# Rotary embedding on one core: alignment instructions on two engines, and the first batch's stores cut 4, 12 and 16 KB

## The chip, the cores and the metric

The kernel runs on one core of a Trainium2 chip. A core has TensorE (PE), VectorE (DVE), ScalarE (ACT), GpSimd (POOL) and SyncE (SP), and 16 DMA engines that move data between HBM and the on-chip memory. The metric is the device time of one execution in microseconds (us); smaller is better. Before the change the median of three runs is 163.62 us (163.49 to 163.76).

## The reference

```python
def reference(x, cos, sin):
    x1 = x[..., : x.shape[-1] // 2]
    x2 = x[..., x.shape[-1] // 2 :]
    cos = cos[None, :, None, :]
    sin = sin[None, :, None, :]
    out1 = x1 * cos - x2 * sin
    out2 = x1 * sin + x2 * cos
    return np.concatenate([out1, out2], axis=-1)
```

`x` is 8 x 2048 x 8 x 64 (batch, position, head, width) in float32, 33.55 MB; `cos` and `sin` are 2048 x 32. Each head's two halves are rotated by the angle of its position. Every element is read once and written once.

## The kernel before

**Tiling.** Each of the 8 batches is one tile `xt`, 128 partitions by 8192 elements: a partition holds 16 consecutive positions, 32 KB in one contiguous row of HBM. There are five such buffers (`NBUF`); the result is written over the input in the same buffer, and stored from there. `HD` is 512 elements (2 KB, one position), `UNIT` is 2048 elements (8 KB, four positions).

**Loads.** All go to SyncE's queue (lines 66 to 69). Batch 0 comes in three parts, with rows of 8, 8 and 16 KB, and the cosine table after the first of them; every later batch is one transfer of 128 rows of 32 KB. The sine table is the first transfer of ScalarE's queue (line 76). The loads of batches 0 to 4 are issued at the start, and the load of batch b + 5 after batch b in the program, where it waits for the store of batch b, whose buffer it takes.

**Work.** `rotate` handles one piece, usually 2048 columns. GpSimd makes the sine products in two instructions (line 122), VectorE the cosine products in one (line 129), and for most pieces (kind A) VectorE adds the two (line 136). For five first pieces of a batch (kinds B and C) TensorE adds through an identity matrix `eye`, and ScalarE copies the sum back (lines 143 to 168); in kind C VectorE makes the sine products as well (line 148). `eye` is made by GpSimd at the start (lines 80 and 81), and ScalarE derives the negated tables from it and from the sine table (lines 90 to 92).

**Stores.** Batches 0 to 6 are stored through ScalarE's queue, batch 7 through SyncE's (line 73). Batch 0 is computed in pieces of 2, 2, 4, 4 and 4 positions (`pieces`), and stored in two transfers (`shares`), the first when 4096 columns are done, that is after its third piece. Batches 1 to 6 are one store each, with rows of 32 KB. Batch 7 is stored in three transfers, with rows of 16, 8 and 8 KB.

**Order.** Nearly every instruction is wrapped in `keep`, so each engine runs them in the order of the program text. The semaphores that tell of a transfer's landing are eight and are handed out in rotation, so that some transfers wait for an earlier one with the same semaphore.

Of the kernel before, what the change touches and what calls it, by code (L numbers as in the profile page):

```python
# [10 lines left out]
def kernel(  # L11
# [7 lines left out]
    nc = tc.nc  # L19
    keep = tc.keep_in_program_order  # L20
# [6 lines left out]
    HD = H * D  # L27
    R = S // P
    ROW = R * HD
    UNIT = 4 * HD  # L30
# [20 lines left out]
    eye = const_pool.tile([P, P], f32, tag="eye")  # L51
# [25 lines left out]
    for b in range(NBUF):  # L77
        load(b)

    nc.gpsimd.memset(eye, 0.0)  # L80
    nc.gpsimd.affine_select(
        out=eye,
        in_=eye,
# [92 lines left out]

    def shares(b):
        if b == 0:
            return [2 * UNIT, 2 * UNIT]
        if b == last:  # L180
            return [2 * UNIT, UNIT, UNIT]
        return [ROW]

    for b in range(B):
        done = 0
        outs = list(spans(shares(b)))
        for lo, n in spans(pieces(b)):
            rotate(b, lo, n)
            done = lo + n
            while outs and sum(outs[0]) <= done:  # L190
                store(b, *outs.pop(0))
        if b + NBUF <= last:
            load(b + NBUF)
# [30 lines left out]
```

## Time and profile before

| quantity | value |
|---|---|
| median of 3 runs | 163.62 us |
| span of the profiled execution, first to last instruction | 161.8 us |
| what the median has beyond the span | 1.8 us |
| read from HBM, written to HBM | 34.08 MB, 33.55 MB |
| mean rate over the span | 418 GB/s |
| VectorE's last addition ends | 156.02 us |

The time of the profiled execution itself is not given apart from its span, so the difference of 1.8 us stands for what lies before and after it. In the chain of work that ended last, the transfers have 48% of the span, VectorE 37%, GpSimd 9%:

```profile
DMA 48%; DVE 37%; POOL 9%; issue 2%; DVEq 0%; SPq 0%; POOLq 0%; ACTq 0%
```

The main groups of instructions are GpSimd's two products and VectorE's product and addition. The columns are line, engine, operation, output and inputs, count; then busy time and mean length in ns; then the engine's idle time before them and what ended it:

```profile
L122 POOL TENSOR_TENSOR t<-xt,sin_sb 128x1024 f32<-128x1024 f32 (+1 forms) x32 | 70.4, 2199 | 13.5 <-DMA xt<-in_x_dram 8.3
L129 DVE TENSOR_TENSOR t<-xt,cos_ps 128x2048 f32<-128x2048 f32 (+1 forms) x34 | 73.4, 2167 | 0.8
L136 DVE TENSOR_TENSOR xt<-t,t 128x2048 f32<-128x2048 f32 (+1 forms) x29 | 62.2, 2145 | 8.2 <-POOL t L122 5.5
```

The transfers by issuing queue, with the size of each and the median time from issue to landing:

```profile
xt<-in_x_dram SPq DMA_DIRECT2D x7, 4096.0 KB, 42.8
out_dram<-xt ACTq DMA_DIRECT2D x6, 4096.0 KB, 27.2
out_dram<-xt ACTq DMA_DIRECT2D x2, 2048.0 KB, 22.3
out_dram<-xt SPq DMA_DIRECT2D x1, 2048.0 KB, 9.9
out_dram<-xt SPq DMA_DIRECT2D x2, 1024.0 KB, 6.2
```

### The profile page before, as it was taken

The numbers are of one execution on the slowest core, as the hardware profiler recorded it, in microseconds if no ns is written. First come the engines' busy times: TensorE is split into PE (matmuls) and PEld (weight loads), VectorE is DVE, ScalarE is ACT, GpSimd is POOL, SyncE is SP. The second block draws the span as 40 slices with busy tenths as digits, with TensorE's granted clock in tenths as the row PEclk, the third lists the DMA queues.
The fourth block names the chain that finished last, engine by engine and source line by source line (L and its number), as shares of the span: only waits on it lengthen the run. The fifth ranks groups of instructions, "written<-read, shape, count | busy, mean of one in ns | idle before, by whom it ended". The sixth has DMA issues, their size and how long they took to land.

```text
span 161.8 us, 459 instructions
## 1 busy us (share of the span) xinstructions
PE 49.4 (31%) x80; PEld 18.5 (11%) x80; DVE 140.1 (87%) x66; ACT 12.8 (8%) x14; POOL 138.9 (86%) x70
## 2 busy tenths in 40 slices
PE   0000000597309760978049714972000000000000
PEld 0000000142004220322023301330000000000000
DVE  0297999999999999999999999199989999899950
ACT  3300000002200220021000220022000000000000
POOL 1399997998999999992999959999899997999800
PEclk9999999999975998589957995699655555555555
DMA  5999999999999999899899999999999999999995
GB/s 158 425 454 494 413 308 446 413 470 405 462 405 462 389 502 405 389 510 397 389 510 397 389 512 397 397 502 397 397 488 413 405 478 413 405 478 409 397 419 225
DMA packets 3314, 67.65 MB, mean 418 GB/s; under 512 B 368, under 2 KB 368, under 8 KB 624
## 3 DMA queue, kind: packets, MB, share of 16 engines
q1 hardware_dynamic: 2016, 38.01, 55.5%
q10 hardware_dynamic: 1296, 29.62, 42.6%
q14 instruction: 2, 0.02, 0.0%
HBM read 34.08 MB, written 33.55 MB: 418 GB/s over the span
## 4 chain that ended last, share of the span: by engine, by line
DMA 48%; DVE 37%; POOL 9%; issue 2%; DVEq 0%; SPq 0%; POOLq 0%; ACTq 0%
DMA xt<-in_x_dram 26%; DVE t L129 18%; DMA out_dram<-xt 18%; DVE xt L136 17%; POOL t L122 9%; DMA sin_sb<-in_sin_dram 4%; DVE t L148 1%; DVEq L136 0%; SPq L67 0%; POOLq L122 0%; ACTq L74 0%
## 5 line engine op out<-in xcount | busy, mean ns | idle before, releaser
L122 POOL TENSOR_TENSOR t<-xt,sin_sb 128x1024 f32<-128x1024 f32 (+1 forms) x32 | 70.4, 2199 | 13.5 <-DMA xt<-in_x_dram 8.3
L129 DVE TENSOR_TENSOR t<-xt,cos_ps 128x2048 f32<-128x2048 f32 (+1 forms) x34 | 73.4, 2167 | 0.8
L122 POOL TENSOR_TENSOR t<-xt,nsin 128x1024 f32<-128x1024 f32 (+1 forms) x32 | 70.3, 2196 | 0.0
L136 DVE TENSOR_TENSOR xt<-t,t 128x2048 f32<-128x2048 f32 (+1 forms) x29 | 62.2, 2145 | 8.2 <-POOL t L122 5.5
L143 PE MATMUL o<-t,eye 128*128 128x512 f32 x24 | 17.0, 799 | 23.1 <-DVE t L129 19.6
L160 PE MATMUL o<-t,eye 128*128 128x512 f32 x16 | 12.0, 844 | 37.8 <-DVE t L129 35.6
L144 PE MATMUL o<-t,eye 128*128 128x512 f32 x24 | 14.9, 709 | 0.0
L145 ACT COPY xt<-o 128x1024 f32<-128x1024 f32 x6 | 6.1, 1012 | 45.7 <-PE o L144 45.7
L143 PEld LDWEIGHTS o<-t,eye 128*128 128x128 f32 x24 | 5.5, 256 | 32.5 <-issue 26.5
L160 PEld LDWEIGHTS o<-t,eye 128*128 128x128 f32 x16 | 3.7, 256 | 43.2 <-issue 39.4
L165 ACT COPY xt<-o 128x1024 f32<-128x1024 f32 x4 | 4.0, 1012 | 47.8 <-PE o L161 47.8
L93 DVE COPY cos_ps<-cos_sb 128x512 f32<-128x512 f32 x1 | 0.7, 695 | 6.9 <-DMA cos_sb<-in_cos_dram 6.9
L144 PEld LDWEIGHTS o<-t,eye 128*128 128x128 f32 x24 | 5.6, 234 | 8.2 <-issue 7.6
L161 PE MATMUL o<-t,neye 128*128 128x512 f32 x8 | 6.3, 875 | 0.2
L148 DVE TENSOR_TENSOR t<-xt,sin_ps 128x2048 f32<-128x2048 f32 x2 | 4.6, 2281 | 0.0
L161 PE MATMUL o<-t,eye 128*128 128x512 f32 x8 | 4.1, 592 | 0.0
L161 PEld LDWEIGHTS o<-t,neye 128*128 128x128 f32 x8 | 2.2, 300 | 5.3 <-issue 3.6
L161 PEld LDWEIGHTS o<-t,eye 128*128 128x128 f32 x8 | 1.5, 190 | 1.9 <-issue 1.9
L90 ACT ACT_TABLE_LOAD x1 | 1.3, 1283 | 1.2 <-PEq L208 1.2
L90 ACT ACTIVATE nsin<-sin_sb 128x512 f32<-128x512 f32 x1 | 0.6, 629 | 4.0 <-DMA sin_sb<-in_sin_dram 4.0
L91 ACT COPY sin_ps<-sin_sb 128x512 f32<-128x512 f32 x1 | 0.6, 580 | 0.0
L80 POOL MEMSET eye<- 128x128 f32 x1 | 0.2, 204 | 0.3 <-POOLq L208 0.3
(6 smaller groups left out, 1.0 us busy)
## 6 DMA issues: line engine op xcount, KB each, us to landing
xt<-in_x_dram SPq DMA_DIRECT2D x7, 4096.0 KB, 42.8
out_dram<-xt ACTq DMA_DIRECT2D x6, 4096.0 KB, 27.2
out_dram<-xt ACTq DMA_DIRECT2D x2, 2048.0 KB, 22.3
xt<-in_x_dram SPq DMA_DIRECT2D x2, 1024.0 KB, 6.7
xt<-in_x_dram SPq DMA_DIRECT2D x1, 2048.0 KB, 12.2
out_dram<-xt SPq DMA_DIRECT2D x1, 2048.0 KB, 9.9
out_dram<-xt SPq DMA_DIRECT2D x2, 1024.0 KB, 6.2
sin_sb<-in_sin_dram ACTq DMA_DIRECT2D x1, 256.0 KB, 5.7
```

Of the source, the lines that this page charges most:

```text
L90: keep(nc.scalar.mul(nsin, sin_sb, -1.0))
L93: keep(nc.vector.tensor_copy(cos_ps, cos_sb))
L122: nc.gpsimd.tensor_mul(out=t2u[:, :, u, :].rearrange("p (r h) d -> p r h d", h=H), in0=xu[:, :, 1 - u, :].rearrange("p (r h) d -> p r h d" ...
L129: nc.vector.tensor_mul(out=t1.rearrange("p (r k d) -> p r k d", r=nr, d=Dh), in0=xk, in1=rep(cos_ps[:, r0 : r0 + nr, :], 2 * H),)
L136: keep(nc.vector.tensor_add(out=xt, in0=t1, in1=t2))
L143: nc.tensor.matmul(oc, eye, t1[:, cs], start=True, stop=False)
L144: nc.tensor.matmul(oc, eye, t2[:, cs], start=False, stop=True)
L145: keep(nc.scalar.copy(xt[:, 2 * j * C : 2 * (j + 1) * C], o))
L148: nc.vector.tensor_mul(out=t2.rearrange("p (r k d) -> p r k d", r=nr, d=Dh), in0=xk, in1=rep(sin_ps[:, r0 : r0 + nr, :], 2 * H),)
L160: nc.tensor.matmul(oc, eye, t1u[:, gs, u, :], start=True, stop=False)
L161: nc.tensor.matmul(oc, eye if u else neye, t2u[:, gs, 1 - u, :], start=False, stop=True)
L165: nc.scalar.copy(xu[:, :, u, :], o.rearrange("p (g d) -> p g d", d=Dh))
```

## The change

VectorE and GpSimd get one alignment instruction each, ahead of all their other work in the kernel. It asks that the next instruction of that engine stand at a multiple of 256 instructions in the engine's program; the room left free is jumped over, not executed. The setting of `eye` to zero is now held in program order too, behind it. The two stores of batch 0, with rows of 16 KB each, become three, with rows of 4, 12 and 16 KB: the first is issued after the first piece, the second after the third piece, where the old first one was, and the last after the fifth as before.

```diff
-    nc.gpsimd.memset(eye, 0.0)
+    for eng in (nc.vector, nc.gpsimd):
+        keep(eng.addr_align(256, max_nops=0))
+    keep(nc.gpsimd.memset(eye, 0.0))
     nc.gpsimd.affine_select(
...
     def shares(b):
         if b == 0:
-            return [2 * UNIT, 2 * UNIT]
+            return [2 * HD, UNIT + 2 * HD, 2 * UNIT]
```

Since there is one transfer more, the semaphores of all later transfers move on by one in the rotation. Lines behind the first edit stand two lower in the changed kernel.

## The prediction

> **What bounds the kernel now.** I read the page first (engines, the span in slices, the queues), then busy time by stretches, then the order of time round the waits, then the transfers at the very end.
>
> ```profile
> span 161.8 us, 459 instructions
> PE 49.4 (31%) x80; PEld 18.5 (11%) x80; DVE 140.1 (87%) x66; ACT 12.8 (8%) x14; POOL 138.9 (86%) x70
> DMA  5999999999999999899899999999999999999995
> q1 hardware_dynamic: 2016, 38.01, 55.5%
> q10 hardware_dynamic: 1296, 29.62, 42.6%
> q14 instruction: 2, 0.02, 0.0%
> ```
>
> VectorE at 87% looks like the bound, but q1 (SyncE's queue: all loads and the last three stores) and q10 (ScalarE's: the sine load and the other stores) together fill 98.1% of the 16 DMA engines. The stretches say where the rest is:
>
> ```profile
> 0.00:4.00 4.00, 0.00 (x0) 0.00 (x0) 0.00 (x0) 1.28 (x1) 0.70 (x6) 1.00 0.54 158
> 4.00:20.00 16.00, 0.00 (x0) 0.00 (x0) 11.83 (x8) 1.35 (x3) 13.47 (x8) 1.00 1.06 452
> 20.00:26.00 6.00, 0.00 (x0) 0.00 (x0) 5.76 (x4) 0.00 (x0) 5.11 (x3) 1.00 0.92 339
> 26.00:52.00 26.00, 13.86 (x20) 5.24 (x21) 25.52 (x12) 2.02 (x2) 25.23 (x11) 0.89 0.99 429
> 52.00:134.00 82.00, 35.50 (x61) 13.29 (x59) 76.21 (x35) 8.10 (x8) 75.81 (x34) 0.75 1.01 434
> ```
>
> Last two columns: DMA share and GB/s. From 26 us on the rate is flat at 429 to 434. Moving 67.65 MB at 434 takes 155.9 us, 5.9 less than the span. Besides the start-up, one loss stands out: 20 to 26 us at 339, just after the first store is issued at 18.36. A row counts where it starts, so I join it to the stretch before: 22 us at (16 x 452 + 6 x 339) / 22 = 421 instead of 434, or 22 x 13 / 434 = 0.65 us; over 4 to 52 us the same reckoning (425) gives 0.95. I use 0.8 us, once.
>
> ```profile
> 18.36 9.79 ACTq L74 DMA_DIRECT2D out_dram<-xt  x2
> 26.04 2.33 POOL L122 TENSOR_TENSOR t<-xt,sin_sb 128x1024 f32<-128x1024 f32 x1 [0.93 <-DMA xt<-in_x_dram]
> 105.13 2.29 DVE L136 TENSOR_TENSOR xt<-t,t 128x2048 f32<-128x2048 f32 x1 [3.57 <-POOL t L122]
> 134.45 2.33 POOL L122 TENSOR_TENSOR t<-xt,sin_sb 128x1024 f32<-128x1024 f32 x1 [1.14 <-DMA xt<-in_x_dram]
> 156.05 0.33 SPq L74 DMA_DIRECT2D out_dram<-xt  x1
> ```
>
> GpSimd waits for loads six times (8.3 us), VectorE for GpSimd after that: the engines follow the transfers. Finally the end, two stretches of transfers (159.6 to 160.2, then 160.2 to 160.8) and the instruction queue between 91 and 95 us:
>
> ```profile
> DMA packets 27, 0.11 MB, mean 191 GB/s; under 512 B 13, under 2 KB 13, under 8 KB 13
> ...
> DMA packets 4, 0.01 MB, mean 14 GB/s; under 512 B 3, under 2 KB 3, under 8 KB 3
> ...
> q14 instruction: 1, 0.01, 0.5%
> ```
>
> The packets under 512 B are the 16 end marks of the last store, one per DMA engine: 13 engines finish before 160.2 us and three after, the last at 160.55. One instruction packet takes 0.005 x 16 x 4 = 0.32 us of one engine; there are two, near 94.4 and 120 us. The last landing sets the end, so a DMA engine that fetched code on the side holds it back. That these three are late because of fetches is inferred.
>
> **The change part by part.** The target is the profiled span, 161.8; the runs' median 163.62 lies 1.8 above it, carried over unchanged.
>
> *The alignment instructions.* Each starts its engine's work at the head of a 256-instruction block. VectorE has 69 rows in its program and GpSimd 76, so the fetches now in mid-run should move to the start or away. Instructions: one on each engine, no row shows one; from below 0, from above the waits that cover it: 6.9 us on VectorE (first work waits for the cosine table) and 5.2 us on GpSimd (for sine). Behind it on GpSimd wait the memset and select of `eye` (done at 1.3 us), needed by ScalarE at 7.53. I take 0; were the cover gone, a jump that had to wait for code would delay both engines by the excess. The fetch: if it leaves the saturated stretch, the last end mark comes back to the pack, from 160.55 to about 160.1: -0.45. If it returns in the first 4 us, its engine may stay 0.32 behind to the end: 0, or +0.1 with a third fetch. The start-up stretch has slack (54% share), so it may be absorbed: I take -0.2.
>
> [...]
>
> *The stores of batch 0.* Before: 16 KB rows after the third and the fifth piece (18.36 and 27.8 us). Now: 4 KB rows after the first piece, whose VectorE add runs from 9.04 to 10.27; then 12 KB and 16 KB at the old times. The DMA engine moves 434 / 16 = 27 KB/us: a 32 KB row costs 1.21 us, 16 KB 0.61, 12 KB 0.45, 4 KB 0.15. With both queues filled it alternates row by row: between the landings of the two old stores (38.05 and 52.6, from issue plus time to landing) lie 14.55 us, or 8 x 1.82 = 8 x (1.21 + 0.61); the following 32 KB store took 19.4 = 8 x 2.42.
>
> So each queued store row holds one load row back by its own length. The old first store needed 3.85 us from issue to its first row (first packet of q10 after 22.1 us, none before). The new one, issued at 10.3 behind 16 KB load rows, should start near 13.4, when the load of xt1 starts. xt1 meets 8 rows of 0.15 = 1.2 us instead of one or two of 0.61: +0.2 (-0.3 to +0.6). xt2 meets 12 KB rows, not 16: -8 x 0.15 = -1.2. xt3 meets 16 KB rows only, where its last pair now meets a 32 KB row: -0.6. From xt3 on, loads land 1.6 earlier; one row's phase either way shifts this by 1 us, so -0.5 to -2.6.
>
> What xt1's delay can hit: GpSimd's factor of the second piece is ready at 32.95, used by VectorE at 34.48 only after its own work, and VectorE begins xt1 at 27.69, 1.7 us after the landing: hidden. The extra issue on ScalarE's queue (0.34 us at 10.3, nothing else there until 18.36) is hidden too. The semaphores of the transfers rotate by one: xt2's load now waits for sine (6.5 us), xt4's for the third part of xt0 (14.3 instead of 9.4), with xt1 filling q1 until 25; hidden by 10 us. The later loads reuse buffers after stores that landed over 20 us before the queue reached them.
>
> The earlier xt7 brings everything after 134.45 forward by 1.6, VectorE's end from 156.02 to 154.4. That is **not** the gain: the DMA engines have the same bytes to move and are full to 160 us, so the last store, issued earlier, queues longer. Only lost DMA time counts. Rows: 8 more per DMA engine, each with the constant part of a row (42.6% of 16 x 161.8 over 29.62 MB against 434 GB/s leaves under 0.01 us a row): +0.06. Gap before the last store, issued at 156.05 just as the one ahead drains: -0.05. The 0.8 us at the opening of the stores: gone at best (-0.8), paid twice at worst (+0.8). Its cause isn't visible; 4 KB rows are a quarter of the burst, and the loads beside them are at first shorter. Nearest row: that one opening. I take a quarter off: -0.2.
>
> Sum: -0.2 + 0 + 0.06 - 0.05 - 0.2 = -0.4: span 161.4, time **163.2**; bounds of this case 162.4 to 163.5.
>
> **The rivals.** *No change, 163.65:* code is fetched at the start instead and the opening costs the same 0.8; +0.06 remains. For it: bytes and rates are equal. Against: the last three end marks.
>
> *Slower, 166.0:* the opening loss belongs to every round in which all 16 DMA engines turn from reading to writing in step. Now it covers two rounds (the two load rows round the first store row), 0.4 each, and the 16 KB rows pull the engines apart; if 4 KB rows do not, all eight rounds pay: 8 x 0.4 - 0.8 = +2.4. It decides from the third round on. For it: the loss lies exactly at the first turn. Against: one opening only to judge by.
>
> *Slower, 164.5:* the queues don't share by rows once rows are small; the store pieces finish early, the first 32 KB store starts 1.8 us sooner (46.3 + 3.85 = 50.2 against 51.9) and puts 0.9 us of rows ahead of xt7, after which GpSimd and VectorE need the same 21.6 us. Against: the exact 8 x 1.82. [...]
>
> *The alignment does not move the fetches, 163.4:* only the stores count.
>
> **How the numbers follow.** Forecast 0.47, no change 0.25, slower by the opening 0.17, slower by the sharing 0.05, no alignment 0.06. Below 163.29 or above 163.95 (0.2%, about what a measurement of this kernel can tell): faster 0.45 (the forecast but for its upper edge), same 0.30 (that edge, no change, no alignment), slower 0.25 (both slow cases and the upper bound of the opening, paid twice). The range takes the lower bound, 162.4, and reaches 164.4, the opening paid twice; beyond it lies most of the 166.0 case.
>
> **What would show it.** Right: first q10 row near 13.4 us; xt3 to xt7 land 0.5 to 2.6 us earlier; VectorE ends near 154.4, yet the last mark moves by under 1 us; no q14 packet between 10 and 155 us; the 16 last marks within 0.5 us. Wrong: a stretch from 12 to 25 us below 380 GB/s, DMA share under 0.95 after 140 us, or VectorE waiting over 0.5 us in batch 1.

## The result, and the profile after

The changed kernel takes 163.96 us (median, 163.58 to 170.46), the kernel before, on the same chips, 163.61. The ratio is 1.0024 with a 95% interval of 1.0015 to 1.0033: it became slower by 0.24%, where 163.2 and faster were forecast. Three of the 22 executions of the changed kernel lasted 168.8 to 170.5 us, and some of two experiments (e5, e10) up to 172; the ratios leave such executions out.

The profiled execution of the changed kernel is its fastest, 163.58 us, so its span equals that of before; three more profiles of the same kernel stand under e13 to e15. The span and the queues, from its page:

```profile
span 161.8 us, 462 instructions
...
q1 hardware_dynamic: 2016, 38.01, 55.3%
q10 hardware_dynamic: 1440, 29.62, 42.7%
q14 instruction: 4, 0.03, 0.1%
```

The same bytes, 144 more packets in q10 (128 rows and 16 end marks of the added store), and four packets of code where there were two. Busy time by stretches (again the last two columns are the DMA share and GB/s):

```profile
4.00:20.00 16.00, 0.00 (x0) 0.00 (x0) 11.70 (x8) 1.35 (x3) 13.40 (x9) 1.00 1.03 434
20.00:26.00 6.00, 0.00 (x0) 0.00 (x0) 5.76 (x4) 0.00 (x0) 5.25 (x3) 1.00 0.98 386
26.00:52.00 26.00, 13.01 (x20) 5.00 (x21) 25.52 (x12) 2.02 (x2) 24.46 (x11) 0.87 1.01 434
52.00:134.00 82.00, 34.48 (x61) 12.81 (x59) 76.32 (x35) 8.10 (x8) 76.53 (x34) 0.75 1.01 434
```

The weak stretch from 20 to 26 us rose from 339 to 386 GB/s and the one behind it from 429 to 434. Over 4 to 52 us the mean is 428 instead of 425. So the transfers lose less in the middle, as hoped, and the time does not show it. The order of time:

```profile
3.51 0.20 POOL L82 MEMSET eye<- 128x128 f32 x1 [3.07 <-issue]
...
10.44 0.34 ACTq L74 DMA_DIRECT2D out_dram<-xt  x1
...
27.54 2.32 POOL L124 TENSOR_TENSOR t<-xt,sin_sb 128x1024 f32<-128x1024 f32 x1 [2.29 <-DMA xt<-in_x_dram]
...
104.88 2.29 DVE L138 TENSOR_TENSOR xt<-t,t 128x2048 f32<-128x2048 f32 x1 [3.20 <-POOL t L124]
...
134.41 2.32 POOL L124 TENSOR_TENSOR t<-xt,sin_sb 128x1024 f32<-128x1024 f32 x1 [1.08 <-DMA xt<-in_x_dram]
...
155.99 0.33 SPq L74 DMA_DIRECT2D out_dram<-xt  x1
```

Three things are to be seen. `eye` is set at 3.51 us instead of 0.73: GpSimd waited 3.07 us for nothing that the profile names. The load of xt1 reaches GpSimd at 27.54 instead of 26.04, after a wait of 2.29 instead of 0.93. And the last load, forecast 1.6 us earlier, releases GpSimd at 134.41 against 134.45, so that the last store is issued at 155.99 against 156.05.

Where the code packets lie shows in the transfers from 1 to 4 us and from 6 to 8 us:

```profile
q14 instruction: 2, 0.02, 2.5%
...
q14 instruction: 2, 0.02, 2.2%
```

By the packet records they start at 1.63, 1.76, 6.71 and 6.73 us; before, the two were at 94.4 and 120.0. The stretches of transfers at the end, 159.2 to 160.2 and 160.2 to 160.8, with the end marks as packets under 512 B:

```profile
DMA packets 38, 0.20 MB, mean 197 GB/s; under 512 B 14, under 2 KB 14, under 8 KB 14
...
DMA packets 4, 0.02 MB, mean 27 GB/s; under 512 B 2, under 2 KB 2, under 8 KB 2
```

Fourteen DMA engines are done by 159.98 us (before: thirteen by 160.08) and two end 0.6 us after them, the last at 160.62 (before: 160.55). In the profiles of the changed kernel and of all experiments, the time of the execution minus its last end mark is 2.96 to 3.15 us (here 163.58 - 160.62 = 2.96). So in all of these the time followed the latest of the 16 DMA engines.

### The profile page after: what moved, and what is told of

Same layout as the page of the kernel before. It is cut to its first block, busy times and chain, and to the rows that moved or that the text cites. A ratio compares the mean times of both kernels' runs of the same rounds, so it can differ in the third digit from the quotient of the medians.

```text
span 161.8 us, 462 instructions
## 1 busy us (share of the span) xinstructions
PE 47.5 (29%) x80; PEld 17.8 (11%) x80; DVE 140.1 (87%) x66; ACT 12.8 (8%) x14; POOL 138.8 (86%) x70
## 4 chain that ended last, share of the span: by engine, by line
DMA 48%; DVE 37%; POOL 9%; issue 2%; DVEq 0%; SPq 0%; POOLq 0%; ACTq 0%
DMA xt<-in_x_dram 26%; DMA out_dram<-xt 19%; DVE t L131 18%; DVE xt L138 17%; POOL t L124 9%; DMA sin_sb<-in_sin_dram 4%; DVE t L150 1%; DVEq L138 0%; SPq L67 0%; POOLq L124 0%; ACTq L74 0%
## 5 line engine op out<-in xcount | busy, mean ns | idle before, releaser
L145 PE MATMUL o<-t,eye 128*128 128x512 f32 x24 | 16.5, 777 | 23.5 <-DVE t L131 20.0
L162 PE MATMUL o<-t,eye 128*128 128x512 f32 x16 | 10.7, 753 | 38.6 <-DVE t L131 36.4
L146 PE MATMUL o<-t,eye 128*128 128x512 f32 x24 | 14.9, 709 | 0.0
L163 PE MATMUL o<-t,eye 128*128 128x512 f32 x8 | 4.1, 592 | 0.0
```

The lines of the kernel that those rows point to most:

```text
L145: nc.tensor.matmul(oc, eye, t1[:, cs], start=True, stop=False)
L146: nc.tensor.matmul(oc, eye, t2[:, cs], start=False, stop=True)
L162: nc.tensor.matmul(oc, eye, t1u[:, gs, u, :], start=True, stop=False)
L163: nc.tensor.matmul(oc, eye if u else neye, t2u[:, gs, 1 - u, :], start=False, stop=True)
```

## The experiments

The records do not name the DMA engine of a packet, but each closes every transfer with its own end mark: in the changed kernel q1's 14 transfers have 224 marks of 4 bytes, q10's 10 have 160, 16 for each. For each profile I list how far the latest mark lies behind the median one when xt0 has landed ("lag"), the last mark of xt7's load, the end of VectorE's last addition, the last mark of all (all in us), and when code packets ran. These four are of one profiled execution; its own time is the last mark plus about 3.0 us and can differ from the median beside it by up to 0.6 us. "New stores" are 4, 12 and 16 KB.

| kernel | time, ratio [95%] | lag at xt0 | xt7 landed | VectorE ends | last mark | code packets at |
|---|---|---|---|---|---|---|
| before | 163.61 | 0.17 | 133.84 | 156.02 | 160.55 | 94.4, 120.0 |
| after | 163.96, 1.0024 [1.0015, 1.0033] | 1.52 | 133.91 | 155.96 | 160.62 | 1.63, 1.76, 6.71, 6.73 |
| e13, e14, e15: the same | 164.48, 163.79, 163.83 | 1.97, 1.13, 1.43 | 134.80, 131.65, 134.15 | 156.86, 153.74, 156.19 | 161.51, 160.78, 160.86 | 1.6 to 1.8, 6.5 to 7.2 |
| e1: new stores alone | 163.41, 0.9995 [0.9986, 1.0005] | 0.47 | 132.30 | 154.37 | 160.29 | 94.0, 118.2 |
| e2: alignment alone | 164.38, 1.0073 [1.0041, 1.0105] | 1.31 | 135.05 | 157.11 | 161.76 | 1.64, 1.77, 6.73, 7.87 |
| e3: on VectorE only | 164.15, 1.0033 [1.0020, 1.0046] | 1.56 | 133.09 | 155.14 | 161.02 | 1.75, 7.43, 118.6 |
| e4: on GpSimd only | 163.52, 1.0015 [0.9996, 1.0033] | 0.67 | 132.27 | 154.36 | 160.42 | 1.78, 6.75, 94.1 |
| e6: offset 216 | 164.47, 1.0048 [1.0036, 1.0060] | 1.02 | 133.43 | 155.56 | 161.35 | 1.76, 3.62, 60.5, 66.0 |
| e7: stepped, not jumped | 165.13, 1.0093 [1.0079, 1.0106] | 2.01 | 132.21 | 155.00 | 162.55 | 6.9, 7.5, 12.1, 13.65 |
| e8: e1 and 2 rows | 163.42, 0.9983 [0.9969, 0.9997] | 0.65 | 132.32 | 154.35 | 160.37 | 96.5, 118.3 |
| e9: e1 and 16 rows | 164.42, 1.0045 [1.0030, 1.0059] | 0.22 | 133.45 | 155.63 | 161.37 | 97.5, 119.2 |
| e12: e1 and 3 times 2 rows | 164.66, 1.0070 [1.0057, 1.0084] | 1.66 | 133.01 | 155.06 | 160.93 | 91.6, 118.2 |
| e11: stores 4, 4, 8, 16 KB | 163.67, 0.9995 [0.9981, 1.0008] | 0.43 | 125.20 | 151.95 | 160.39 | 94.1, 111.0 |

**The two halves (e1, e2).**

```diff
 e1, on the kernel before:
-            return [2 * UNIT, 2 * UNIT]
+            return [2 * HD, UNIT + 2 * HD, 2 * UNIT]
 e2, on the kernel before:
+    for eng in (nc.vector, nc.gpsimd):
+        keep(eng.addr_align(256, max_nops=0))
+    keep(nc.gpsimd.memset(eye, 0.0))
```

> Only the stores of batch 0 changed (rows of 4, 12 and 16 KB), no alignment. Theory A (the alignment costs: in the changed kernel GpSimd waits 3.07 us for code at the start, and two code packets of 8 KB at 6.7 us fall on two DMA engines that are then full and stay behind): ratio to before 0.996 to 1.000, the last end marks of xt1's load within 0.7 us of their median instead of 2.25 us, no instruction packets before 10 us, two in mid-run as before. Theory B (the small rows cost): ratio 1.002 to 1.004, with xt1's end marks as far apart as in the changed kernel. Both expect the stretch from 20 to 28 us to lose less than the 0.85 us of before.

> Only the two alignment instructions, stores of batch 0 as before (16 and 16 KB). Theory A: ratio 1.002 to 1.005, a wait of about 3 us before GpSimd sets eye, instruction packets near 1.7 and 6.7 us and none in mid-run, two DMA engines more than 1.5 us behind the median in xt1's end marks, a wider scatter of times than before. Theory B: ratio 0.998 to 1.001, because the start has room and the mid-run packets are gone.

The stores alone cannot be told from the kernel before (0.9995); the alignment alone costs 0.73%, 1.2 us, more than was expected. Two of its nine executions took 166.1 and 166.3 us and weigh on that; the median of the other seven, 164.37, is 0.48% or 0.8 us above the kernel before. With the new stores in place the alignment costs 1.0024 - 0.9995 = 0.29%, 0.47 us, and those two intervals do not overlap. The ends of e1, 159.0 to 160.2 and 160.2 to 160.8:

```profile
DMA packets 45, 0.25 MB, mean 212 GB/s; under 512 B 14, under 2 KB 14, under 8 KB 14
...
DMA packets 2, 0.00 MB, mean 0 GB/s; under 512 B 2, under 2 KB 2, under 8 KB 2
```

After 160.2 us only two end marks are left and no data. The ends of e2, 160.2 to 161.2 and 161.2 to 162.0:

```profile
DMA packets 31, 0.14 MB, mean 139 GB/s; under 512 B 14, under 2 KB 14, under 8 KB 14
...
DMA packets 3, 0.01 MB, mean 10 GB/s; under 512 B 2, under 2 KB 2, under 8 KB 2
```

The median mark is at 160.56, 0.6 us later than before (159.95), and two engines are later still, up to 161.76. That the fourteen are late too has a cause upstream: xt7 lands 1.2 us later than before (135.05), VectorE ends 1.1 us later, and the last store is issued that much later. So the late DMA engines act twice: by their own end, and by every load, which counts as landed only when the slowest engine has brought its rows (in the changed kernel xt7's median mark is at 130.76 us, its last at 133.91, and the load's landing at 134.28).

**Which engine's alignment (e3, e4, e5).**

```diff
 on the changed kernel:
-    for eng in (nc.vector, nc.gpsimd):
+    for eng in (nc.vector,):                                  # e3
+    for eng in (nc.gpsimd,):                                  # e4
+    for eng in (nc.vector, nc.gpsimd, nc.scalar, nc.tensor):  # e5
```

> New stores, alignment on VectorE alone. Theory A: one pair of instruction packets at the start and one late DMA engine instead of two; ratio between that of the stores alone and 1.0024, that is 1.000 to 1.002; one instruction packet left in mid-run (GpSimd's). If the engine does not matter, this and the GpSimd one come out alike. Theory B: 1.002 to 1.004 as in the whole change.

> New stores, alignment on GpSimd alone. Theory A: 1.000 to 1.002, one late DMA engine, a wait of about 3 us before GpSimd sets eye, one packet left in mid-run (VectorE's). Theory B: 1.002 to 1.004.

> The whole change, with alignment instructions on ScalarE and TensorE too (the suspected cost doubled). Theory A (each aligned engine jumps into a block of code that is not there, and has it fetched at 1.7 us and the following one near 7 us, when the DMA engines are full; the DMA engine that carries the second packet loses about 1 us and stays behind): up to four packets near 1.7 us and four near 7 us, three or four DMA engines over 1 us behind in xt1's end marks, ratio to before 1.003 to 1.008. Rival (only VectorE's and GpSimd's start matters, or the scatter has nothing to do with code): 1.002 to 1.003, as the whole change.

VectorE's alone costs 0.38% over e1, above what was expected, GpSimd's alone 0.20%, with intervals that overlap. The packet records show a difference: behind the second code packet the next row of 8 KB took 0.97 us in e3 and 0.66 in e4, instead of 0.31. e4's twelve times fall into two groups, seven at 163.30 to 163.53 and five at 164.25 to 164.65; its profile is of the first group, with a lag of 0.67 only. So the same program may cost nothing or 1 us from one execution to the next. Four aligned engines (e5) give 1.0082 [1.0048, 1.0115] from four of seven executions (164.00 to 166.02); the profile, which is one of the others (171.34), has six code packets from 1.7 to 10.1 us. That more code packets early cost more is likely by this, but how much each adds is not settled.

**Without the long jump (e6, e7).**

```diff
 on the changed kernel:
-        keep(eng.addr_align(256, max_nops=0))
+        keep(eng.addr_align(256, offset=216, max_nops=0))   # e6
+        keep(eng.addr_align(256))                           # e7
```

e6 aligns to instruction 216 of a block instead of its head; e7 fills the room with idle instructions, which are stepped through and not jumped over.

> The whole change, but both alignment instructions ask for slot 216 of a block instead of slot 0: a shorter padding that should stay inside the block that the engine is already in, with the step into the next block about 40 instructions later. Theory A: no 3 us wait before GpSimd sets eye, no packets before 10 us, two packets in mid-run (somewhere from 30 to 90 us), ratio 0.998 to 1.001, like the stores alone. Rival (the instruction or its padding costs by itself): 1.002 to 1.004 as the whole change.

> The whole change, with the padding executed as idle instructions instead of jumped over. Theory A, if the miss comes from the jump: no wait of 3 us for code, since the next block is fetched while the padding runs, and a second packet that comes earlier or not at all before 10 us; ratio 0.998 to 1.001. Theory A, if the miss comes from the step into the next block however it is made: packets near 1.7 to 3 us and 7 us again, ratio 1.002 to 1.004. The rival of small rows gives nothing new here.

e6 was meant as the same instruction without a fetch, and its 0.998 to 1.001 were missed at 1.0048. GpSimd did start early:

```profile
1.17 0.20 POOL L82 MEMSET eye<- 128x128 f32 x1 [0.72 <-POOLq L210]
```

But in the transfers from 1 to 5 us there are again two code packets:

```profile
q14 instruction: 2, 0.02, 1.6%
```

With those at 60.5 and 66.0 that makes four, as in the changed kernel. Whose the early two are is not shown. One DMA engine has a lag of 1.02 at xt0. At xt3 it is 2.11, at xt4, after the packets in mid-run, 3.02, and the last end mark comes at 161.35, 1.73 behind the median. So GpSimd's 3 us of waiting are not needed for the loss, and a part of the loss, about 0.7 to 0.9 us of lag, came in mid-run. e7 goes further. It executes 188 idle instructions on GpSimd (until 8.52 us) and 189 on VectorE (until 9.99), and its order of time has

```profile
8.90 0.20 POOL L82 MEMSET eye<- 128x128 f32 x1 [8.46 <-issue]
...
153.77 1.23 DVE L138 TENSOR_TENSOR xt<-t,t 128x1024 f32<-128x1024 f32 x1
```

GpSimd's first work comes at 8.90 us, well past the cover of 5.2 us, and the first store is issued at 13.74 instead of 10.44. Yet VectorE's last addition ends at 155.00, 1.0 us before that of the kernel before. The time is the worst of all comparisons (1.0093), because of the last stretch, 161.5 to 162.8 us:

```profile
DMA packets 5, 0.02 MB, mean 19 GB/s; under 512 B 2, under 2 KB 2, under 8 KB 2
```

Two DMA engines are still moving rows there; code packets had run as late as 12.1 and 13.65 us, amid full queues (q1 alone has 97% of the 16 DMA engines from 11 to 15 us). This refutes the rival that the time is lost by VectorE or GpSimd beginning late: in e3, e6 and e7 VectorE ends 0.5 to 1.0 us before the kernel before and the last mark comes 0.5 to 2.0 us after its 160.55.

**A late DMA engine without any code (e8, e9, e10, e12).** Here DMA engines are held back by data: by a load of 2 rows of 8 KB on ScalarE's queue, behind the sine table, or by one of 16 rows. The load of 2 rows adds two end marks, so two DMA engines carry it (from 0.5 to 15 us e8 has 82 packets under 512 B, e1 has 80); behind the load of 16 rows all 16 are late alike, to within 0.25 us (e9). The loaded rows are used by nothing.

```diff
 e8 on e1, e10 on the kernel before; e9 the same with 16 for 2:
+    spare = t2_pool.tile([2, 4 * HD], f32, tag="t2")
+    keep(nc.scalar.dma_start(out=spare, in_=xv[last, 0:2, 0 : 4 * HD]))
 e12 on e1:
+    for i, pool in enumerate((t2_pool, t1s_pool, t1s_pool)):
+        spare = pool.tile([2, 4 * HD], f32, tag="t1s" if i else "t2", name=f"spare{i}")
+        keep(nc.scalar.dma_start(out=spare, in_=xv[last, 0:2, 4 * HD * i : 4 * HD * (i + 1)]))
```

> No alignment; the new stores, and one extra load of two rows of 8 KB, issued on ScalarE's queue right behind the first use of the sine table (about 7 us), so that two of the 16 DMA engines carry 8 KB more each, the size of a code packet; the data is not used. Theory A (what counts is that single DMA engines fall behind early): two DMA engines 0.3 to 1.1 us late in xt0's last part, 1.5 to 3 us in xt7; ratio to before 1.001 to 1.004, that is 0.15 to 0.45% over the stores alone (0.9995). Rival C (the alignment costs through VectorE and GpSimd starting late or through their waits for code, not through the DMA engines): 0.999 to 1.0005, like the stores alone.

> The same with 16 rows of 8 KB, one for every DMA engine: eight times the bytes, but no engine is late against the others. By bytes alone (16 x 8 KB at 434 GB/s) 0.3 us, ratio 0.19% over the stores alone, 1.0010 to 1.0020. Theory A: not dearer than the two rows, though it moves eight times as much. If the bytes counted and not the lateness, this one would cost eight times what the two rows cost.

> The two extra rows with the old stores of batch 0 (16 and 16 KB). Theory A: two DMA engines late as before; xt7's landing moves out to 134.9 to 136 us, because without the new stores the loads have no lead to spend, and the end with it: ratio 1.003 to 1.007, above the two rows with the new stores. Rival C: 1.000 to 1.001.

> No alignment; the new stores and three extra loads of two rows of 8 KB each, issued one behind the other at about 7 us, so that two DMA engines carry 24 KB more each: 3 x 0.31 = 0.93 us of rows and what the turn to a second queue costs, near the 1.0 to 1.5 us by which the DMA engines with a code packet are late in xt0's last part. The data is not used. Theory A (one or two DMA engines about 1 us behind from the start are enough, whatever put them there): the two are 1 to 1.6 us late in xt0's last part and 2 to 3.2 us in xt7, the last end mark comes 0.3 to 1 us later than with the stores alone (160.29), ratio to before 1.001 to 1.005. Rival D (a late DMA engine alone costs nothing, as the two single rows did; the code packets cost in another way): 0.998 to 1.000.

e8 cost nothing: its three latest DMA engines are only 0.44 to 0.65 us behind at xt0 (e1 has one, 0.47 behind). The theory of the late DMA engine had expected 1.001 to 1.004, so it holds only from some size on. e12 tripled it: its two latest DMA engines, taken for the carriers, are 1.54 and 1.66 us behind at xt0, as far as in the changed kernel, and the time is 0.70% above that of before, with code packets only in mid-run, where e1 has them too; 1.001 to 1.005 had been expected. Its last addition and, from 160.2 to 160.6 and 160.6 to 161.2 us, its last transfers:

```profile
153.84 1.23 DVE L139 TENSOR_TENSOR xt<-t,t 128x1024 f32<-128x1024 f32 x1
```

```profile
DMA packets 4, 0.02 MB, mean 61 GB/s; under 512 B 1, under 2 KB 1, under 8 KB 1
...
DMA packets 3, 0.01 MB, mean 14 GB/s; under 512 B 2, under 2 KB 2, under 8 KB 2
```

VectorE ends at 155.06, earlier than before, and two engines carry rows to the end. This is the signature of the alignment, made without alignment. In part it is more bytes and more issues, but those are 48 KB of 67.65 MB, 0.11 us if all 16 DMA engines shared them.

e9 was to show what the same extra rows cost when all engines share them: by bytes 128 KB, 0.31 us, 0.19%. It took 0.50% more than e1. Up to xt5 the latest mark stays within 0.25 us of the median, and all engines are late, in xt0's last part by 1.5 us. The stretches from 10 to 14 and from 14 to 20 us, of e9 and then of e1:

```profile
10.00:14.00 4.00, 0.00 (x0) 0.00 (x0) 3.83 (x4) 0.00 (x0) 2.00 (x3) 1.00 0.99 307
14.00:20.00 6.00, 0.00 (x0) 0.00 (x0) 3.13 (x2) 0.00 (x0) 6.00 (x3) 1.00 1.05 448
```

```profile
10.00:14.00 4.00, 0.00 (x0) 0.00 (x0) 3.83 (x4) 0.00 (x0) 4.00 (x4) 1.00 1.13 484
14.00:20.00 6.00, 0.00 (x0) 0.00 (x0) 5.13 (x3) 0.00 (x0) 6.00 (x3) 1.00 0.93 399
```

Together that is 392 GB/s against 433, and 10 x 41 / 434 = 0.9 us. From 10 to 14 us e9's DMA engines are busy (0.99) and move little: in the packet records, 16 KB rows that start near 11 us take mostly 1.4 to 1.7 us, where others take 0.61. Not all of that is left at the end, where e9's median mark is 0.6 us behind e1's (160.37 against 159.76). The rest of the 1.1 us between the last marks came in mid-run: behind the code packet at 97.5 us a 32 KB row took 1.79 us instead of 1.21, and from xt6's load to the end one DMA engine is 1.00 behind the median. So e9 does not price the extra rows alone, and it shows one DMA engine made late by a single code packet in mid-run. For e10 there is no ratio: its times run from 163.43 to 169.79 with a median of 166.59. It is inconclusive, and a lag without code on the old stores was not measured otherwise.

**Is the opening of the stores worth anything (e11)?**

```diff
 on the kernel before:
-            return [2 * UNIT, 2 * UNIT]
+            return [2 * HD, 2 * HD, UNIT, 2 * UNIT]
```

> No alignment; batch 0 stored as rows of 4, 4, 8 and 16 KB, the second after the second piece. If the loss at the opening of the stores (0.85 us of DMA time before, 0.4 with rows of 4, 12 and 16 KB) comes from the size of the step from short to longer rows while all DMA engines are in step, it falls to 0.1 to 0.3 us and the ratio is 0.997 to 0.999, faster than both kernels. If it does not depend on it, 0.999 to 1.0005, like the stores alone.

Over 4 to 52 us the mean rate is 431.5 GB/s against 425 before and 428 in e1; by (434 - rate) / 434 x 48 us the loss is 0.3 us, against 1.0 and 0.7. The loads run 8.6 us ahead of those of the kernel before, and VectorE ends 4.1 us earlier:

```profile
150.72 1.23 DVE L136 TENSOR_TENSOR xt<-t,t 128x1024 f32<-128x1024 f32 x1
```

The time is the same, 0.9995 [0.9981, 1.0008]; 0.997 to 0.999 were expected. In the last 3 us all 16 marks fall, up to 160.39:

```profile
DMA packets 44, 0.23 MB, mean 76 GB/s; under 512 B 16, under 2 KB 16, under 8 KB 16
```

This is the plainest evidence that an earlier end of VectorE does not shorten the time. Nor was the loss at the opening gone: from 52 to 134 us e11 has 430 GB/s where the others have 434, and 82 x 4 / 434 is 0.8 us. A window counts a row where it starts, so the rows themselves tell it better. Added up over 18 to 52 us and shared among 16 DMA engines, the time by which 32 KB rows last longer than their usual 1.21 us is 0.8 us before, 0.5 in e1 and 0.6 in e11, there from 33 to 50 us. All rows together take 158.5, 158.3 and 158.3 us per DMA engine, so the mean engine gains only about 0.2 us by either opening.

**How much the changed kernel scatters (e13, e14, e15).** The changed kernel, unchanged, three more profiles.

> The changed kernel itself, one more look. In all profiles so far the time of the profiled execution is the last end mark of the last store plus 2.96 to 3.15 us. Theory A: the time lies between 163.6 and 164.7; the last end mark is the time less 3.0; the one or two latest DMA engines are late (over 0.9 us) from xt0's last part on, behind code packets near 7 us. In an execution near the median (163.96) the last mark lies near 160.95, 0.6 us or more behind the second group of DMA engines. Against it: a run near or over the median in which all end marks lie within 0.5 us, or in which the late DMA engine was on time until 20 us.

> A second such look, with the same expectation: it tells whether the scatter of the changed kernel's times goes with how far the carriers of the code packets are behind.

> A third such look, with the same expectation as the first: the time is the last end mark plus 3.0 us, and the last DMA engine is one that was late from xt0's last part on.

The end marks of e13, 160.2 to 160.65 and 160.65 to 161.6 us:

```profile
DMA packets 17, 0.02 MB, mean 37 GB/s; under 512 B 15, under 2 KB 15, under 8 KB 15
...
DMA packets 3, 0.02 MB, mean 17 GB/s; under 512 B 1, under 2 KB 1, under 8 KB 1
```

Here one DMA engine alone, 1.97 us behind at xt0, holds the end to 161.51. In e14 xt7 lands at 131.65 and VectorE ends at 153.74, 2.3 us earlier than before, and the execution takes 163.79 all the same. Four times the code packets came at the same places to within 0.7 us, and the lag at xt0 was 1.13 to 1.97: the scatter of the changed kernel is, by this, that of its late DMA engine. The lag at xt0 and the time go together only roughly (after: 1.52 and 163.58; e14: 1.13 and 163.79). The lag at the last store goes with the time better: 0.73, 1.09, 1.10 and 1.20 us for 163.58, 163.79, 163.83 and 164.48, where in e13 the last store was late as well, as in e2.

## Why the prediction was wrong

**The failed step is the fetch: "I take -0.2", within -0.45 and +0.1, the fetch from which "its engine may stay 0.32 behind to the end".** The alignment measured +0.47 us with the new stores and +0.8 to +1.2 us alone. Two parts of the step failed, when the code comes and what a packet costs; a third held only in part.

- *When the code comes.* The forecast put it in the first 4 us, where the DMA engines have slack (share 0.54 before). One pair of packets did come at 1.63 and 1.76 us and was mostly absorbed: at xt0's first part the latest mark is 0.45 us behind the median, 0.17 in the kernel before. A second pair came at 6.71 and 6.73 us, when the DMA engines are full (share 1.03 from 4 to 20 us).
- *What a packet costs.* The 0.32 us is the packet alone. In the packet records the next row behind it, the one that starts as it ends, is stretched too, and so it was in the kernel before: behind the two packets in mid-run, rows of 32 KB took 1.56 and 1.43 us instead of 1.21, so that the two cost their DMA engines 0.66 and 0.53 us. That fits the two latest marks there, 0.60 and 0.53 behind the median. In the changed kernel, beside the 8 KB rows at 7 us, the packets took 0.36 and 0.34 us and the rows behind them 0.95 and 0.96 instead of 0.31: about 1 us each. With one engine aligned, the row behind VectorE's packet was longer than that behind GpSimd's, one packet each: 0.97 (e3) against 0.66 (e4) for 8 KB rows, and where one engine alone was left to fetch in mid-run, 1.75 (e4: VectorE) against 1.43 (e3: GpSimd) for 32 KB rows. Why a row is stretched is open.
- *What a late DMA engine costs.* That it stays behind to the end was right, with another size: at the last store the lag is 0.73 us here and 1.09 to 1.20 in e13 to e15, against 0.54 in e1. What the forecast left out is the loads between. Their lag grows from 1.52 us at xt0 to 2.26 at xt1 and 3.15 at xt7, so that xt7's load, landed when the latest engine is done, gives up the lead of the stores, and in e2 and e13 the last store is issued late by it. The likely reason for the growth is the alternation by rows that the forecast used itself (14.55 us for 8 rows of 1.21 and 8 of 0.61): an engine that is late finds one more store row to serve before its load row. That is argued, not tried, and the growth needs no code: in e1 the lag goes from 0.47 to 1.69, at no cost. e12 shows a cost of this size with no code packet before 91 us.

**The jump itself, taken as 0 under a cover of 5.2 and 6.9 us: right.** The branch on GpSimd is at 0.69 us, its next instruction at 3.5, within the cover: GpSimd's first product starts at 6.67 instead of 6.53, VectorE's table copy at 7.11 instead of 6.93. The first two code packets run between the two, from 1.63 to 2.43 us; that GpSimd waited for code is inferred from this order. In e7, which steps through the room, the first two packets ran at 6.9 and 7.5 us, while both engines still executed idle instructions, and GpSimd's and VectorE's next instructions came 0.4 us after the last of these, against 2.8 us behind GpSimd's jump in the changed kernel. What the forecast did not ask is what the packets cost the DMA engines that carry them.

**The stores, -0.19 in sum: right within the error.** e1 measured -0.05%, -0.08 us, with an interval of -0.23 to +0.08. The signs came out nearly to the number in e1: xt1's last mark came 0.23 us later (25.57 to 25.80; +0.2 forecast), xt7 1.54 earlier (1.6 forecast), VectorE ended at 154.37 (154.4 forecast). In the changed kernel the lag covers them: xt7's median mark came 2.35 us earlier, 130.76 against 133.11, and its last mark 0.07 later. Of the 0.8 us at the opening about 0.3 to 0.4 came back (-0.2 taken), and 4 KB and 12 KB rows took 159 and 460 ns against the estimates of 0.15 and 0.45. The first row was at 13.94, for 13.4 forecast.

**The bound: right.** "That is not the gain" is what e11 shows with 4.1 us.

**The move of the mid-run fetches: right.** No code packet lies between 10 and 155 us, in this profile and in e13 to e15. The other sign, all last marks within 0.5 us, failed: they spread from 159.40 to 160.62, because the code came early on. None of the signs of being wrong showed: 12 to 25 us had 439 GB/s, the DMA share from 140 to 160 us was 0.96, and VectorE waited for nothing in batch 1. All three look at means or at VectorE, and none at the latest DMA engine.

**The rivals.** *No change* named the right place, the code fetched at the start, and priced it at nothing. *166.0 by the opening in all eight rounds* did not happen: the stretches to 26 us move as much as before (16 x 434 + 6 x 386, over 22, is 421). *164.5 by sharing not by rows* did not either: the medians of the first three stores end at 24.6, 38.3 and 52.8 us, one by one, in rounds of a load row and a store row: they lie 13.6 and 14.5 us apart, where 8 rounds of 1.21 + 0.46 and of 1.21 + 0.61 make 13.4 and 14.6. The case that came, a DMA engine that carries code amid full queues and keeps the rest waiting, was in the bound of +0.1 and not among the rivals.

The best version measured is e1, the stores without the alignment. It is not distinguishable from the kernel before, and no run here beats that one beyond doubt: e8, with an interval of 0.9969 to 0.9997, is e1 with two useless rows, and I do not take its 0.17% for an effect. Open are why the row behind a code packet is stretched, and whether more behind VectorE's; why e4's times fall into two groups; and which DMA engine carries the code.

## What to carry to other kernels

Where all DMA engines are full, look at the last one, not at the mean: here 1.0 to 2.0 us lost by one or two of sixteen in the first 15 us went with 0.2 to 0.9% of the time. What a packet on the side costs is to be read with the row behind it: here, from 6.5 us on, 0.31 to 0.36 us for the packet and 0.2 to 0.7 us more for the row. The code packets here held up rows of data, so an edit of the program's layout belongs in the transfers' account: ask when its packets come and beside which rows. And a load's mark by the median tells little: here xt7's median mark lay 3.15 us before its last, and GpSimd, which waited for the load, began 0.50 us after the last.

## What the runs showed of the hardware that was not expected

- A code packet took 0.31 us in mid-run and 0.31 to 0.36 at 6.5 to 7.9 us, and the row behind it was stretched: 8 KB rows to 0.58 to 0.97 us instead of 0.31, 32 KB rows to 1.43 to 1.79 instead of 1.21, in e3 and e4, with one packet each, more behind VectorE's (0.97 and 1.75) than behind GpSimd's (0.66 and 1.43).
- With one engine aligned to the head of a block, two code packets came early (e3: 1.75 and 7.43 us; e4: 1.78 and 6.75): about the first, an aligned GpSimd sat idle for 2.9 to 4.3 us (e4 and e5; 3.07 in the changed kernel), about the second the trace shows no wait.
- 16 rows of 8 KB on a second queue beside the opening loads put all DMA engines 1.5 us back at 15 us and 0.6 us at the end, where their bytes ask for 0.3 (e9 against e1).
- A lag of up to 0.65 us on three DMA engines cost nothing (e8), one of 1.54 and 1.66 us on two cost 1.2 us (e12 over e1).
